# One triangular solve for both chunk pairs of an RWKV group, and the last group's solve on VectorE

## The chip, the cores and the metric

The kernel runs on one core of a Trainium2 chip. The metric is the device time of one execution in microseconds (us); lower is better. A core has a matrix engine (TensorE, PE in the profile, its weight loads PEld), three engines for elementwise work (VectorE, DVE; ScalarE, ACT; GpSimd, POOL), and an engine that issues DMAs (SyncE, SP). Each engine takes its own instructions strictly in order and waits on semaphores for the others.

## The reference

The kernel computes two layers of a backbone over 512 latent tokens and 256 context tokens, width 1024. Each layer is a half-step SwiGLU, a token mixer and another half-step SwiGLU. The mixer projects once, runs four branches (attention, bidirectional RWKV-7, pooling, a 2-D Fourier transform), and projects their concatenation. The change is in the RWKV branch, a recurrence over a 64x64 state S for each of four heads and two directions:

```
def step(S, inp):
    r_t, w_t, k_t, v_t, a_t, b_t = inp
    sa = jnp.einsum('bhvk,bhk->bhv', S, a_t)
    S = S * w_t[:, :, None, :] + sa[..., None] * b_t[:, :, None, :] + v_t[..., None] * k_t[:, :, None, :]
    y = jnp.einsum('bhvk,bhk->bhv', S, r_t) if emit else None
    return S, y
...
rw_c, finals = rwkv_mix(rwkv_prepare(zc[3], zc[4], zc[5], zc[6], p), (zero, zero), p, emit=ctx_out)
rw_l, _ = rwkv_mix(rwkv_prepare(zl[3], zl[4], zl[5], zl[6], p), finals, p, emit=True)
```

The context sequence C is run first; its final states start the latent sequence L. In the last layer the context's output isn't needed.

## The kernel before

The recurrence is computed in chunks of 64 positions. Inside a chunk the steps depend on each other through a unit triangular 64x64 matrix for each head and direction, which has to be inverted; between chunks only S is handed on. The work of a layer is cut into three groups of 256 positions: C, and L in two halves; direction 0 runs forward and direction 1 backward, so the first L group takes positions 0 to 255 forward and 256 to 511 backward (`off` is (0, 256)), the second the reverse (`off` is (256, 0)). A group has four chunks, in two pairs (`cp` 0 and 1).

Per group, `group_start` computes the decays. Per pair, `group_pair` (L907 to L985) builds the scaled vectors `AR` and `BK`, multiplies them on PE to the matrices `gram` (evicted and masked by DVE, L956), writes the negated 32x32 diagonal blocks into `NTX` (ACT, L960), and transposes keys and values into `bkT` and `uv`.

`group_solve` (L987) inverts the 32 diagonal blocks of a pair (8 head-and-chunk combinations, 2 directions, 2 blocks). `M` holds the blocks four times, on the partitions 0 to 31, 32 to 63 and so on (two DVE transposes, L998 and L1001, a copy on ACT, one on POOL). `X` in the tile `Xs` is the inverse; row t is kept by partition group t mod 4. Then 31 steps run, j from 31 down to 1, each a multiply (L1011) and an add (L1013) on the rows from j//4 on: (8 - j//4) times j elements on each partition. Each of the 62 instructions needs the one before it. They run on POOL, except in the first pair of the second L group (`late`), on DVE. Behind it, X is copied into `NTX` (L1016, ACT and POOL) and transposed (L1019, L1020, DVE), the 64x64 inverse is put together by two small products on PE (`pm1`, L1030, and `pm2`, L1047) with ACT between, and 16 small copies write it into `gram` (L1042, ACT and POOL).

`chain` (L1052) carries S through a pair's two chunks: PE computes z from S (L1068, L1071), ACT copies it to `Wz`, PE multiplies by the inverse (L1077), DVE and ACT evict `uv` (L1082, L1080), PE makes the update (L1088), DVE adds it to S and scales it (L1090, L1091), and PE, ACT and DVE make the output y (L1097 to L1105). A chain step needs the previous S and its pair's solve; 12 steps make a layer.

Attention (`attend`) is a list of pieces that `fill(n)` emits n at a time: scores psc (L1226), maxima (L1228), exponentials, transposes ppT (L1247), products po (L1253). `fill(FILL[l][nth])` takes two pieces at each of six places, `fill(100)` the rest. `rwkv_out` makes the normalised output of the branch.

The program is given to a scheduler: instructions come in program order, with a higher priority inside `with hot()`, and a timeline that the scheduler keeps for itself sets the order of each engine at build time. So where a line stands in the program decides only in part where its instruction stands in its engine's queue. In `mixer`, before: both C pairs are prepared and solved one after the other, then pooling and Fourier, then the two C chains; in the L groups, each pair is prepared, solved, and followed by two pieces of attention and the chain of the previous pair. The last pair's chain comes after the loop.

Of the kernel before, what the change touches and what calls it, by code (L numbers as in the profile page):

```python
# [13 lines left out]
ALU = mybir.AluOpType  # L14
# [35 lines left out]
FILL = ((2,) * 6, (2,) * 6)  # L50
# [3 lines left out]
class K:  # L54
# [856 lines left out]
    def group_pair(self, R, G, cp):  # L911

        nc = self.nc
        s, off, emit = G["s"], G["off"], G["emit"]
        nx = 2 if emit else 1
        AR = self.slot([128, 2, 2, 2, 2, 64], name="AR")
        BK = self.slot([128, 2, 2, 2, 2, 64], name="BK", tag="w")
        A = self.slot([128, 32, 32], name="NTX", tag="w")
        NT = A[64:96]
        ch = slice(128 * cp, 128 * cp + 128)  # L920
        cq = "p f (c q) -> p f c q"
        mul = lambda o, a, b: nc.vector.tensor_tensor(o, a, b, op=ALU.mult)
        H = {"G": G, "cp": cp, "gram": [], "A": A, "AR": AR, "late": s == "L" and off[0] and not cp}
        for d in range(2):
            D = G["D"][d]

# [13 lines left out]
            if emit:  # L940
                r = R[s, "r"]
# [5 lines left out]
            p = [self.ps([128, 2, 2, 128], "pgr", "rk") for _ in range(2)]  # L947
# [36 lines left out]
                    nc.gpsimd.tensor_tensor(D["kds"], D["kds"], D["kd"], op=ALU.add)  # L984
        return H  # L985

    def group_solve(self, H):  # L987


        nc = self.nc  # L990
        A = H["A"]
        X1T, XT, NT = A[0:32], A[32:64], A[64:96]
# [10 lines left out]
        X, tmp, Pm = XS[:, 0:256].rearrange("p (t i) -> p t i", i=32), XS[:, 256:512], XS[:, 512:768].rearrange("p (u t) -> p u t", t=32)  # L1003
        nc.gpsimd.memset(XS[:, 0:256], 0.0)
        for x in range(4):
            nc.gpsimd.memset(XS[32 * x:32 * x + 32, x:256:36], 1.0)
# [7 lines left out]
        for x in range(4):  # L1014
            eng = nc.scalar.copy if x % 2 else nc.gpsimd.tensor_copy
            eng(XT[:, :, x::4], X[32 * x:32 * x + 32].rearrange("p t i -> p i t"))  # L1016
        Xb = M[0:32].rearrange("p (x t) u -> p x t u", x=4)
        for x in range(4):
            nc.vector.transpose(Xb[:, x].rearrange(fl), X[32 * x:32 * x + 32].rearrange(fl))  # L1019
        nc.vector.transpose(X1T.rearrange(fl), XT.rearrange(fl))  # L1020

        X1T2, Xb2 = A[64:96], M[64:96].rearrange("p (x t) u -> p x t u", x=4)
        nc.scalar.copy(X1T2[:, :, 8:16], X1T[:, :, 8:16])
        nc.scalar.copy(M[64:96, :, 24:32], M[0:32, :, 24:32])
        X1, X2 = (X1T, X1T2), (Xb, Xb2)
        p = self.ps([128, 8, 32], "pm1", "sv")
        for u in range(8):
            for d in range(2):
                r = slice(64 * d, 64 * d + 32)
                nc.tensor.matmul(p[r, u], H["gram"][d][r, u, 32:64], X1[d][:, :, 8 * d + u], start=True, stop=True)  # L1030
        for d in range(2):
            r = slice(64 * d, 64 * d + 32)
            nc.scalar.mul(Pm[r], p[r], -1.0)
        for d in range(2):
            gr = H["gram"][d]
            nc.gpsimd.memset(gr[64 * d + 32:64 * d + 64, :, 0:32], 0.0)
            for b in range(2):
                us = slice(16 * b + 8 * d, 16 * b + 8 * d + 8)
                r = slice(64 * d + 32 * b, 64 * d + 32 * b + 32)
                for x in range(4):  # L1040
                    eng = nc.gpsimd.tensor_copy if x % 2 else nc.scalar.copy
                    eng(gr[r, :, 32 * b + x:32 * b + 32:4], Xb[:, x, :, us].rearrange("p t u -> p u t"))  # L1042
        p = self.ps([128, 8, 32], "pm2", "sv")
        for u in range(8):
            for d in range(2):
                r = slice(64 * d, 64 * d + 32)
                nc.tensor.matmul(p[r, u].rearrange("p (t x) -> p x t", x=4), Pm[r, u], X2[d][:, :, :, 16 + 8 * d + u], start=True, stop=True)  # L1047
        for d in range(2):
            r = slice(64 * d, 64 * d + 32)
            nc.scalar.copy(H["gram"][d][r, :, 32:64], p[r])  # L1050

    def chain(self, R, H, final):  # L1052

# [362 lines left out]
    def mixer(self, l, h, to_hC, done, last, back, nxt):  # L1416
# [41 lines left out]
        def fill(n):  # L1458
            for _ in range(n):
                next(todo, None)  # L1460
# [6 lines left out]
            att["C"] = t[:, 0]  # L1467
        todo = (x for st in emit[::-1] for x in self.attend(F, st, att))
        mixes["L", 0] = att["L"]
        prev = None  # L1470
        nth = 0
        for H in Hs:
            with hot():
                self.chain(R, H, False)
            fill(FILL[l][nth])
            nth += 1
        for s, off, em in (("L", (0, 256), True), ("L", (256, 0), True)):
            if s == "L" and off[0] == 0:
# [283 lines left out]
```

## Time and profile before

| | |
|---|---|
| three runs | 3124.56, 3129.62, 3129.33 us (median 3129.33) |
| the profiled execution, its span | 3129.89 us, 3128.1 us |
| mean granted clock of TensorE | 0.931 |
| busy share of the span: PE, DVE, ACT, POOL | 93%, 74%, 42%, 17% |
| POOL busy | 531.4 us |

The page's busy shares are averages over the whole span. Most of the span is the SwiGLU products, where POOL has little to do; POOL's work stands in two places, the mixers of the two layers. What a change in the mixers does is read from these stretches. The granted clock is 1.00 or 0.50 at any moment; a value between them is the mean over a stretch.

### The profile page before, as it was taken

Reading aid. Unit: us, or ns where it says so; the run is one execution under the profiler, and the core shown is the slowest. Engines: PE = TensorE matmul, PEld = TensorE weight load, DVE = VectorE, ACT = ScalarE, POOL = GpSimd, SP = SyncE. Lnnn points to the kernel's source line nnn. Section 1 sums busy time; section 2 is a strip of 40 time slices with the busy share of each in tenths; the row PEclk is TensorE's granted clock in tenths of the full one; section 3 lists DMA queues with packets and bytes.
Section 4 is the critical chain, followed back from the end, with each engine's and each line's share of the span. In section 5 each row is a group of like instructions: output and inputs, shape, how many; then the busy total and the mean of one; then the engine's idle time right before and its main releaser. Section 6 shows DMA issues by size and latency. Waiting matters only on the chain.

```text
span 3128.1 us, 50276 instructions
## 1 busy us (share of the span) xinstructions
PE 2910.2 (93%) x20031; PEld 2544.1 (81%) x20031; DVE 2303.3 (74%) x3989; ACT 1313.6 (42%) x2208; POOL 531.4 (17%) x1117
## 2 busy tenths in 40 slices
PE   7999999999888889999998999999999897879997
PEld 5999998787555679999987999998877565679996
DVE  7879998744666768678778889777834566797887
ACT  4433332433676354333325443332433676354443
POOL 2000002103774030000022000001112764010002
PEclk8999999999686999999999999999999677889998
DMA  6334445320001213233232344434420002033332
GB/s 237 103 116 147 135 140 167 125 66 1 30 28 36 89 60 128 95 108 102 95 122 68 103 141 142 135 122 138 146 67 1 23 29 87 34 111 101 108 109 101
DMA packets 92187, 304.60 MB, mean 97 GB/s; under 512 B 13636, under 2 KB 15920, under 8 KB 91952
## 3 DMA queue, kind: packets, MB, share of 16 engines
q1 hardware_dynamic: 91952, 301.39, 29.2%
q8 instruction: 157, 2.57, 0.3%
q14 instruction: 78, 0.64, 0.1%
HBM read 279.81 MB, written 21.54 MB: 96 GB/s over the span
## 4 chain that ended last, share of the span: by engine, by line
PE 73%; DVE 13%; ACT 7%; issue 3%; DMA 2%; POOL 2%; SPq 0%; DVEq 0%; ACTq 0%; POOLq 0%
PE pab L123 8%; PE pab L124 8%; PE pab L125 8%; PE py L123 6%; PE py L124 6%; PE py L125 6%; PE pgu L123 4%; PE pgu L124 4%; PE pgu L125 4%; PE pw L123 2%; PE pw L124 2%; PE pw L125 2%; DVE wlo L119 2%; DVE raw L420 1%; PE pwo L125 1%
## 5 line engine op out<-in xcount | busy, mean ns | idle before, releaser
L118 ACT CAST whi<-raw 128x1024 fp32r<-128x1024 f32 x488 | 507.8, 1050 | 552.5 <-PE py L125 193.1
L119 DVE TENSOR_TENSOR wlo<-raw,whi 128x1024 fp32r<-128x1024 f32 x488 | 600.6, 1239 | 125.3 <-PE py L124 25.5
L123 PE MATMUL pab<-hshi,whi 128*128 128x256 f32 x1408 | 401.3, 288 | 24.5 <-ACT hshi L118 9.7
L124 PE MATMUL pab<-hslo,whi 128*128 128x256 f32 x1408 | 404.7, 288 | 8.9 <-DVE hslo L119 8.9
L125 PE MATMUL pab<-hshi,wlo 128*128 128x256 f32 x1408 | 401.8, 287 | 1.6 <-DVE wlo L119 1.5
L524 POOL TENSOR_TENSOR acc<-acc,gate 128x512 f32<-128x512 f32 x44 | 73.6, 1695 | 1631.0 <-DMA gate<-gate 1167.1
L123 PE MATMUL pab<-h,whi 128*128 128x256 f32 x1056 | 298.7, 287 | 9.7 <-DVE eab L463 7.4
L124 PE MATMUL pab<-h,whi 128*128 128x256 f32 x1056 | 301.6, 287 | 4.6 <-POOL h L317 4.5
L123 PE MATMUL pgu<-hhiC,whi 128*128 128x256 f32 x1056 | 299.7, 284 | 2.8 <-ACT h L286 2.2
L125 PE MATMUL pab<-h,wlo 128*128 128x256 f32 x1056 | 299.9, 286 | 1.9 <-DVE wlo L119 1.9
L124 PE MATMUL pgu<-hloC,whi 128*128 128x256 f32 x1056 | 299.5, 284 | 0.0
L125 PE MATMUL pgu<-hhiC,wlo 128*128 128x256 f32 x1056 | 299.1, 283 | 0.0
L123 PEld LDWEIGHTS pab<-hshi,whi 128*128 128x128 f32 x1408 | 273.3, 196 | 29.3 <-ACT hshi L118 11.2
L123 PE MATMUL py<-whi,actL 128*128 128x512 f32 x704 | 277.2, 395 | 11.0 <-DVE acc L513 8.3
L124 PEld LDWEIGHTS pab<-hslo,whi 128*128 128x128 f32 x1408 | 275.4, 196 | 11.9 <-DVE hslo L119 11.6
L125 PEld LDWEIGHTS pab<-hshi,wlo 128*128 128x128 f32 x1408 | 274.5, 196 | 3.1 <-DVE wlo L119 2.6
L124 PE MATMUL py<-wlo,actL 128*128 128x512 f32 x704 | 276.8, 393 | 0.0
L125 PE MATMUL py<-whi,actL 128*128 128x512 f32 x704 | 274.8, 391 | 0.0
L123 PEld LDWEIGHTS pab<-h,whi 128*128 128x128 f32 x1056 | 202.8, 194 | 15.9 <-DVE eab L463 8.1
L124 PEld LDWEIGHTS pab<-h,whi 128*128 128x128 f32 x1056 | 205.3, 194 | 9.3 <-POOL h L317 6.3
L125 PEld LDWEIGHTS pab<-h,wlo 128*128 128x128 f32 x1056 | 204.8, 195 | 4.1 <-DVE wlo L119 2.5
L123 PEld LDWEIGHTS pgu<-hhiC,whi 128*128 128x128 f32 x1056 | 202.8, 192 | 6.2 <-ACT h L286 2.7
(473 smaller groups left out, 6586.8 us busy)
## 6 DMA issues: line engine op xcount, KB each, us to landing
raw<-in_w_ffn_in SPq DMA_DIRECT2D x176, 512.0 KB, 3.6
rawm<-in_w_mod SPq DMA_DIRECT2D x128, 512.0 KB, 3.7
raw<-in_w_ffn_out SPq DMA_DIRECT2D x88, 512.0 KB, 3.5
raw<-in_w_in SPq DMA_DIRECT2D x24, 512.0 KB, 4.5
back<-spill SPq DMA_DIRECT2D x44, 256.0 KB, 4.3
spill<-res SPq DMA_DIRECT2D x16, 512.0 KB, 7.3
spill<-acc SPq DMA_DIRECT2D x16, 512.0 KB, 3.3
raw<-in_w_out SPq DMA_DIRECT2D x16, 512.0 KB, 3.5
```

Source lines behind the costliest of these rows:

```text
L118: self.nc.scalar.copy(hi, src)
L119: self.nc.vector.tensor_tensor(lo, src, hi.bitcast(F32), op=ALU.subtract)
L123: nc.tensor.matmul(out, st[0], mv[0], start=start, stop=False)
L124: nc.tensor.matmul(out, st[0], mv[1], start=False, stop=False)
L125: nc.tensor.matmul(out, st[1], mv[0], start=False, stop=stop)
L420: nc.vector.tensor_tensor(o, x, y, op=ALU.subtract)
L524: nc.gpsimd.tensor_tensor(a[:, sl], a[:, sl], self.gate[s][:, sl], op=ALU.mult)
```

## The change

Both pairs of a group are solved together. `X` has 16 rows of 32 on each partition, and row t is kept by partition group t mod 2, of 64 partitions, one half of them for each pair. A step works on (16 - j//2) times j elements. `M` holds the blocks twice for each pair (one DVE transpose a pair, then ACT copies to the other 64 partitions). The small gram copies are 32x128 instead of 32x64, and half as many. The engine is an argument: POOL for C and the first L group, DVE for the second.

In the mixer the solve comes after both pairs. The C chains move into the first L group's loop, each behind a pair; each group's chains run in the next group's loop, and the last group's two chains after the loops. `fill(FILL[l][nth])` is called four times a layer.

```diff
-        M = w([128, 32, 32], "M")
-        nc.vector.transpose(M[0:32].rearrange(fl), NT.rearrange(fl))
-        nc.scalar.copy(M[32:64], M[0:32])
-        nc.gpsimd.tensor_copy(M[64:96], M[0:32])
-        nc.vector.transpose(M[96:128].rearrange(fl), NT.rearrange(fl))
+        Ms = [w([128, 32, 32], "M")]
+        M = Ms[0]
+        for cp, H in enumerate(Hs):
+            nc.vector.transpose(M[32 * cp:32 * cp + 32].rearrange(fl), H["A"][64:96].rearrange(fl))
+        nc.scalar.copy(M[64:128, 16:32], M[0:64, 16:32])
+        nc.scalar.copy(M[64:128, 0:16], M[0:64, 0:16])
...
-        eng = nc.vector if H["late"] else nc.gpsimd
         for j in range(31, 0, -1):
-            a = j // 4
-            tv = tmp[:, 0:(8 - a) * j].rearrange("p (t i) -> p t i", i=j)
-            eng.tensor_tensor(tv, M[:, j:j + 1, 0:j].to_broadcast([128, 8 - a, j]),
-                              X[:, a:8, j:j + 1].to_broadcast([128, 8 - a, j]), op=ALU.mult)
-            eng.tensor_tensor(X[:, a:8, 0:j], X[:, a:8, 0:j], tv, op=ALU.add)
-        for x in range(4):
-            eng = nc.scalar.copy if x % 2 else nc.gpsimd.tensor_copy
-            eng(XT[:, :, x::4], X[32 * x:32 * x + 32].rearrange("p t i -> p i t"))
+            a = j // 2
+            tv = tmp[:, 0:(16 - a) * j].rearrange("p (t i) -> p t i", i=j)
+            eng.tensor_tensor(tv, M[:, j:j + 1, 0:j].to_broadcast([128, 16 - a, j]),
+                              X[:, a:16, j:j + 1].to_broadcast([128, 16 - a, j]), op=ALU.mult)
+            eng.tensor_tensor(X[:, a:16, 0:j], X[:, a:16, 0:j], tv, op=ALU.add)
+        Ms.append(w([128, 32, 32], "M"))
...
+            nc.gpsimd.tensor_copy(XT[:, :, 0::2], Xc[0].rearrange("p t i -> p i t"))
+            nc.scalar.copy(XT[:, :, 1::2], Xc[1].rearrange("p t i -> p i t"))
...
             for cp in range(2):
                 Hs.append(self.group_pair(R, g, cp))
-                self.group_solve(Hs[cp])
+            self.group_solve(Hs, nc.gpsimd)
...
-        prev = None
         nth = 0
-        for H in Hs:
-            with hot():
-                self.chain(R, H, False)
-            fill(FILL[l][nth])
-            nth += 1
         for s, off, em in (("L", (0, 256), True), ("L", (256, 0), True)):
...
+            prev, Hs = Hs, []
             g = self.group_start(P, R, s, off, em, first)
             for cp in range(2):
-                H = self.group_pair(R, g, cp)
-                self.group_solve(H)
+                Hs.append(self.group_pair(R, g, cp))
                 fill(FILL[l][nth])
                 nth += 1
-                if prev:
-                    with hot():
-                        self.chain(R, prev, False)
-                prev = H
+                with hot():
+                    self.chain(R, prev[cp], False)
+            self.group_solve(Hs, nc.vector if off[0] else nc.gpsimd)
...
         with hot():
+            self.chain(R, Hs[0], False)
             rw = mixes["L", 1] = self.slot([128, 2, SEQ], name="mixL")[:]
             self.rwkv_out(P, R, "L", rw, (1, 2), "rk")
-            self.chain(R, prev, True)
+            self.chain(R, Hs[1], True)
             self.rwkv_out(P, R, "L", rw, (0, 3), "rk")
```

The instruction counts of the program fall from 1010 to 590 on POOL, from 3798 to 3783 on DVE, from 1958 to 1930 on ACT and from 17090 to 17054 on PE; SP keeps its 657.

Where the instructions stand in their engine's queue is shown at three places. A row is the instruction's number on its engine, its line, its operation and tiles (with buffer numbers), and its shape. The first is POOL in the first L group of layer 0, in the middle of the solves, before:

```order
306 L1011 TENSOR_TENSOR Xs_8292<-M_8287,Xs_8292 128x66
307 L1011 TENSOR_TENSOR Xs_8540<-M_8535,Xs_8540 128x69
308 L1013 TENSOR_TENSOR Xs_8292<-Xs_8292 128x6x11
309 L1013 TENSOR_TENSOR Xs_8540<-Xs_8540 128x3x23
310 L1011 TENSOR_TENSOR Xs_8292<-M_8287,Xs_8292 128x60
311 L1011 TENSOR_TENSOR Xs_8540<-M_8535,Xs_8540 128x66
312 L1013 TENSOR_TENSOR Xs_8292<-Xs_8292 128x6x10
```

The same place of the changed kernel, POOL in the solve of the first L group:

```order
187 L1010 TENSOR_TENSOR Xs_8260<-M_8255,Xs_8260 128x96
188 L1012 TENSOR_TENSOR Xs_8260<-Xs_8260 128x4x24
189 L1010 TENSOR_TENSOR Xs_8260<-M_8255,Xs_8260 128x115
190 L1012 TENSOR_TENSOR Xs_8260<-Xs_8260 128x5x23
191 L1010 TENSOR_TENSOR Xs_8260<-M_8255,Xs_8260 128x110
192 L1012 TENSOR_TENSOR Xs_8260<-Xs_8260 128x5x22
193 L1010 TENSOR_TENSOR Xs_8260<-M_8255,Xs_8260 128x126
```

Before, the steps of two pairs (`Xs_8292`, `Xs_8540`) alternate, so a step has another pair's step between itself and the one it needs. Now there is one solve, and each row needs the row above it.

The second place is PE in layer 0 where attention ends. Before, behind the last `po` (L1253) come the rest of the second L group's second chunk and then two chunk steps; `pch_9895` is the third chunk's z:

```order
5262 L1253 MATMUL po_10110<-pexp_10032,vqC_7588 64x128
5263 L1253 MATMUL po_10110<-pexp_10033,vqC_7588 64x128
5264 L237 MATMUL gps_10180<-ident,modC_498 8x128
5265 L1088 MATMUL pch_9820<-uv_9035,bkT_9034 64x64 x8
5266 L1097 MATMUL pch_9820<-S_859_6193,AR_8989 64x128 x2
...
5275 L1100 MATMUL pch_9820<-uv_9035,gram_9008 64x64
5276 L1068 MATMUL pch_9895<-prm_858_6192,AR_9417 64x128 x2
```

Now, behind the last `po` (L1259) come both pairs' small products of the second L group's solve (L1035, L1052) and then all four of its chunk steps; `pch_9207` is the first chunk's z:

```order
5171 L1259 MATMUL po_9804<-pexp_9726,vqC_7486 64x128
5172 L1259 MATMUL po_9804<-pexp_9727,vqC_7486 64x128
5173 L237 MATMUL gps_9874<-ident,modC_498 8x128
5174 L1035 MATMUL pm_1263_9115<-NTX_8531,gram_8548 32x32
...
5206 L1052 MATMUL pm_1264_9170<-M_9029,Xs_9034 32x2x16 x16
5207 L1052 MATMUL pm_1264_9170<-M_9100,Xs_9034 32x2x16 x16
5208 L1077 MATMUL pch_9207<-uv_8575,gram_8548 64x64
```

Four chunk steps and a solve's products stand behind attention instead of two chunk steps. In layer 1 the last `po` moves from the second L group's first chunk step into the first L group's third.

The third place is DVE in layer 0, in the solve of the second L group. Before, it is the solve of that group's first pair; in its first half it stands among the second pair's gram evictions (L956):

```order
1205 L1013 TENSOR_TENSOR Xs_9064<-Xs_9064 128x28
1206 L956 TENSOR_TENSOR gram_9436<-pgr_9426,prm_858_6192 128x512
1207 L1011 TENSOR_TENSOR Xs_9064<-M_9059,Xs_9064 128x54
1208 L956 TENSOR_TENSOR gram_9436<-pgr_9427,prm_858_6192 128x512
1209 L1013 TENSOR_TENSOR Xs_9064<-Xs_9064 128x2x27
```

Now it is the solve of both pairs; what stands between the steps is attention's maxima (L1234), the evictions of `uv` (L1088) and the updates of S (L1096, L1097) of the first L group's chain:

```order
1303 L1010 TENSOR_TENSOR Xs_9034<-M_9029,Xs_9034 128x121
1304 L1012 TENSOR_TENSOR Xs_9034<-Xs_9034 128x11x11
1305 L1010 TENSOR_TENSOR Xs_9034<-M_9029,Xs_9034 128x110
1306 L1012 TENSOR_TENSOR Xs_9034<-Xs_9034 128x11x10
1307 L1096 TENSOR_TENSOR prm_858_6192<-S_859_6193,pch_9002 64x4x64 x2
1308 L1010 TENSOR_TENSOR Xs_9034<-M_9029,Xs_9034 128x108
1309 L1097 TENSOR_TENSOR prm_858_6192<-prm_858_6192,PC_7748 64x4x64 x2
1310 L1012 TENSOR_TENSOR Xs_9034<-Xs_9034 128x12x9
```

The update with `pch_9002` is that of the first L group's fourth chunk; 18 steps of the solve stand behind it.

## Rows read from the trace of the kernel before

**Rows 1.** Busy us (count): PE, PEld, DVE, ACT, POOL, then PEclk, by stretch.
```profile
760.00:1036.00 276.00, 228.76 (x2055) 167.12 (x2056) 176.92 (x456) 179.21 (x406) 158.43 (x467) 0.74 0.08 27
2420.00:2646.00 226.00, 191.42 (x1706) 138.83 (x1705) 139.38 (x353) 155.25 (x340) 147.06 (x460) 0.71 0.08 28
```

**Rows 2.** Chain of waits, 740 to 1060 us: its shares by engine and line.
```profile
by line: PE po L1253 4.9%; PE psc L1226 4.5%; issue 3.8%; POOL Xs L1011 3.7%; POOL Xs L1013 3.6%; PE ppT L1247 3.3%; PE pw L123 2.7%; PE pw L124 2.7%; PE pw L125 2.6%; DVE gram L956 2.5%; ACT gram L1042 2.5%; ACT pexp L1232 2.4%; ACT NTX L9
```

**Rows 3.** PE's waits, 760 to 1036 us: total, times, longest us.
```profile
PE ppool L1299 <- DVE pooled L1296: 12.8, 2, 9.6
```

**Rows 4.** The tile Xs, whole span: duration ns min/median/max, first and last start.
```profile
L1011 POOL TENSOR_TENSOR Xs<-M,Xs x310: 199/293/1272, 785.4 to 2625.2; 128x60 f32<-128x60 f32 x16, 128x28 f32<-128x28 f32 x10, 128x48 f32<-128x48 f32 x10, 128x54 f32<-128x54 f32 x9
...
L1011 DVE TENSOR_TENSOR Xs<-M,Xs x62: 169/231/391, 935.9 to 2615.8; 128x60 f32<-128x60 f32 x6, 128x28 f32<-128x28 f32 x4, 128x54 f32<-128x54 f32 x4, 128x48 f32<-128x48 f32 x4
```

**Rows 5.** Timeline of POOL (start us, us, what): one solve, two solves, one solve.
```profile
798.39 0.32 POOL L1011 TENSOR_TENSOR Xs<-M,Xs 128x76 f32<-128x76 f32 x1
798.79 0.39 POOL L1013 TENSOR_TENSOR Xs<-Xs 128x76 f32<-128x76 f32 x1
...
816.78 0.51 POOL L1011 TENSOR_TENSOR Xs<-M,Xs 128x48 f32<-128x48 f32 x2
817.23 0.52 POOL L1013 TENSOR_TENSOR Xs<-Xs 128x48 f32<-128x48 f32 x2
...
874.86 0.27 POOL L1011 TENSOR_TENSOR Xs<-M,Xs 128x48 f32<-128x48 f32 x1
875.20 0.28 POOL L1013 TENSOR_TENSOR Xs<-Xs 128x48 f32<-128x48 f32 x1
```

**Rows 6.** Timeline of DVE, the solve in layer 0, first and last steps.
```profile
935.88 0.17 DVE L1011 TENSOR_TENSOR Xs<-M,Xs 128x31 f32<-128x31 f32 x1
936.09 0.19 DVE L1013 TENSOR_TENSOR Xs<-Xs 128x31 f32<-128x31 f32 x1
...
970.75 0.37 DVE L1011 TENSOR_TENSOR Xs<-M,Xs 128x28 f32<-128x28 f32 x1
...
972.65 0.17 DVE L1013 TENSOR_TENSOR Xs<-Xs 128x8 f32<-128x8 f32 x1
```

**Rows 7.** Timeline of DVE: second pairs' M transposes, C and first L group.
```profile
805.08 1.24 DVE L1001 STREAM_TRANSPOSE M<-NTX 32x1024 f32<-32x1024 f32 x1
...
886.48 1.24 DVE L1001 STREAM_TRANSPOSE M<-NTX 32x1024 f32<-32x1024 f32 x1
...
2445.00 1.24 DVE L1001 STREAM_TRANSPOSE M<-NTX 32x1024 f32<-32x1024 f32 x1
...
2524.71 1.24 DVE L1001 STREAM_TRANSPOSE M<-NTX 32x1024 f32<-32x1024 f32 x1
```

**Rows 8.** Timeline of POOL: the copy right behind a solve's last step.
```profile
845.50 1.31 POOL L1016 COPY NTX<-Xs 32x256 f32<-32x256 f32 x2
...
921.84 1.32 POOL L1016 COPY NTX<-Xs 32x256 f32<-32x256 f32 x2
...
2489.14 1.31 POOL L1016 COPY NTX<-Xs 32x256 f32<-32x256 f32 x2
```

**Rows 9.** Timeline of PE: Wz products of late chunk steps, last attention product.
```profile
946.69 0.68 PE L1077 MATMUL pch<-Wz,gram 64*64 64x64 f32 x16
...
1025.10 0.68 PE L1077 MATMUL pch<-Wz,gram 64*64 64x64 f32 x16 [2.12 <-ACT Wz L1074]
...
1034.25 0.68 PE L1077 MATMUL pch<-Wz,gram 64*64 64x64 f32 x16
1034.86 1.53 PE L1253 MATMUL po<-pexp,vqC 128*64 128x128 f32 x24
...
1048.48 0.68 PE L1077 MATMUL pch<-Wz,gram 64*64 64x64 f32 x16
...
2654.80 0.68 PE L1077 MATMUL pch<-Wz,gram 64*64 64x64 f32 x16 [0.46 <-ACT Wz L1074]
...
2669.71 0.68 PE L1077 MATMUL pch<-Wz,gram 64*64 64x64 f32 x16
```

More of the change, by code (lines that the diff above doesn't have):

```diff
@@ L922, in group_pair @@
         mul = lambda o, a, b: nc.vector.tensor_tensor(o, a, b, op=ALU.mult)
-        H = {"G": G, "cp": cp, "gram": [], "A": A, "AR": AR, "late": s == "L" and off[0] and not cp}
+        H = {"G": G, "cp": cp, "gram": [], "A": A, "AR": AR}
         for d in range(2):
@@ L985, in group_pair, with group_solve @@
         return H
-    def group_solve(self, H):
+    def group_solve(self, Hs, eng):
         nc = self.nc
-        A = H["A"]
-        X1T, XT, NT = A[0:32], A[32:64], A[64:96]
         fl = "p a b -> p (a b)"
@@ L1014, in group_solve @@
-        for x in range(4):
-            eng = nc.scalar.copy if x % 2 else nc.gpsimd.tensor_copy
-            eng(XT[:, :, x::4], X[32 * x:32 * x + 32].rearrange("p t i -> p i t"))
[L1017 to L1027, printed above, removed]
-            for d in range(2):
[L1029 to L1050, printed above, removed]
+        Ms = [w([128, 32, 32], "M")]
+        M = Ms[0]
+        for cp, H in enumerate(Hs):
+            nc.vector.transpose(M[32 * cp:32 * cp + 32].rearrange(fl), H["A"][64:96].rearrange(fl))
@@ new lines, in group_solve @@
+        nc.scalar.copy(M[64:128, 16:32], M[0:64, 16:32])
+        nc.scalar.copy(M[64:128, 0:16], M[0:64, 0:16])
+        XS = w([128, 1024], "Xs")
+        X, tmp = XS[:, 0:512].rearrange("p (t i) -> p t i", i=32), XS[:, 512:1024]
+        Pm = tmp.rearrange("p (c u t) -> p c u t", c=2, t=32)
+        nc.gpsimd.memset(XS[:, 0:512], 0.0)
+        for y in range(2):
+            nc.gpsimd.memset(XS[64 * y:64 * y + 64, y:512:34], 1.0)
+        for j in range(31, 0, -1):
+            a = j // 2
[3 more added lines that the diff above has]
+            eng.tensor_tensor(X[:, a:16, 0:j], X[:, a:16, 0:j], tv, op=ALU.add)
@@ new lines, in group_solve @@
+        Ms.append(w([128, 32, 32], "M"))
+        X1, X2, Xb = [], [], []
+        for cp, H in enumerate(Hs):
+            X1T, XT, X1T2 = [H["A"][32 * i:32 * i + 32] for i in range(3)]
+            Xc = [X[64 * y + 32 * cp:64 * y + 32 * cp + 32] for y in range(2)]
+            nc.gpsimd.tensor_copy(XT[:, :, 0::2], Xc[0].rearrange("p t i -> p i t"))
+            nc.scalar.copy(XT[:, :, 1::2], Xc[1].rearrange("p t i -> p i t"))
+            v = "p (y t) u -> p y t u"
+            Xb.append(Ms[cp][0:32].rearrange(v, y=2))
+            for y in range(2):
+                nc.vector.transpose(Xb[cp][:, y].rearrange(fl), Xc[y].rearrange(fl))
+            nc.vector.transpose(X1T.rearrange(fl), XT.rearrange(fl))
+            nc.scalar.copy(X1T2[:, :, 8:16], X1T[:, :, 8:16])
+            nc.scalar.copy(Ms[cp][64:96, :, 24:32], Ms[cp][0:32, :, 24:32])
+            X1.append((X1T, X1T2))
+            X2.append((Xb[cp], Ms[cp][64:96].rearrange(v, y=2)))
@@ new lines, in group_solve @@
+        half = [slice(64 * d, 64 * d + 32) for d in range(2)]
+        p = self.ps([128, 2, 8, 32], "pm1", "sv")
+        for cp, H in enumerate(Hs):
+            for u in range(8):
+                for d, r in enumerate(half):
+                    nc.tensor.matmul(p[r, cp, u], H["gram"][d][r, u, 32:64], X1[cp][d][:, :, 8 * d + u], start=True, stop=True)
+        for r in half:
+            nc.scalar.mul(Pm[r], p[r], -1.0)
+        for cp, H in enumerate(Hs):
+            for d in range(2):
+                gr = H["gram"][d]
+                nc.gpsimd.memset(gr[64 * d + 32:64 * d + 64, :, 0:32], 0.0)
+                for b in range(2):
+                    us = slice(16 * b + 8 * d, 16 * b + 8 * d + 8)
+                    r = slice(64 * d + 32 * b, 64 * d + 32 * b + 32)
+                    for y in range(2):
+                        cpy = nc.gpsimd.tensor_copy if y else nc.scalar.copy
+                        cpy(gr[r, :, 32 * b + y:32 * b + 32:2], Xb[cp][:, y, :, us].rearrange("p t u -> p u t"))
@@ new lines, in group_solve @@
+        p = self.ps([128, 2, 8, 32], "pm2", "sv")
+        for cp in range(2):
+            for u in range(8):
+                for d, r in enumerate(half):
+                    nc.tensor.matmul(p[r, cp, u].rearrange("p (t y) -> p y t", y=2), Pm[r, cp, u], X2[cp][d][:, :, :, 16 + 8 * d + u],
+                                     start=True, stop=True)
+        for cp, H in enumerate(Hs):
+            for d, r in enumerate(half):
+                nc.scalar.copy(H["gram"][d][r, :, 32:64], p[r, cp])
@@ L1469, in mixer @@
         mixes["L", 0] = att["L"]
-        prev = None
         nth = 0
-        for H in Hs:
-            with hot():
-                self.chain(R, H, False)
-            fill(FILL[l][nth])
-            nth += 1
         for s, off, em in (("L", (0, 256), True), ("L", (256, 0), True)):
-            if s == "L" and off[0] == 0:
+            if off[0] == 0:
                 for n in ("kds", "Y"):
```

3 lines of the change are left out of this document (removed).

## The prediction

> **What bounds the kernel now.** The page's averages mix stages with other limits, so I start from the table by stretches [rows 1]. The mixers' middle parts, where solves, chains and attention run side by side, are about 760 to 1060 us (layer 0) and 2420 to 2700 us (layer 1). Up to the last attention product TensorE (PE) is busy 228.8 of 276 us in layer 0 and 191.4 of 226 us in layer 1, at a granted clock of 0.74 and 0.71, a mix of both levels; VectorE (DVE) and ScalarE (ACT) are busy for 62 to 69%, GpSimd (POOL) for 57 to 65%. No engine is full. PE is the nearest to it, with 47 and 35 us idle. The chain of waits in layer 0 agrees [rows 2]: the solve's two lines on POOL hold 7.3% of 320 us, some 23 us; attention's products (po, psc, ppT) hold more. And 12.8 us of PE's idle time belong to a wait for the pooling branch's `pooled` [rows 3], which no edit here touches. So there are two bounds: the serial cycle "pairs, solve, chain", and PE's own work with the gaps it must have.
>
> **The solve's steps.** Before, ten solves on POOL and two on DVE make 620 and 124 step instructions, by the counts 310 and 62 for the multiply line and as many for the add [rows 4]. Afterwards four are on POOL and two on DVE, 248 and 124, each instruction longer. Row j of one kind works on (8 - j//4)·j elements before, at most 76, 1560 in a solve; on (16 - j//2)·j after, at most 136, 2856 in a solve. A step alone on POOL goes from start to start in 0.34 us at 48 elements and 0.40 at 76 [rows 5]: 0.06 us for 28 elements, about 2 ns each. With 92 elements on average (2856/31) that is 0.34 + 0.002·44 = 0.43 us a step, 27 us for 62. Inserted POOL work (copies, memsets, the `kdsL` add) adds some 4 in C and 8 in the first L group: I take 31 and 35 us. Below, a step of the 48-element length would give 62·0.34 = 21; above, if each step were lengthened by as much again as its own 0.27 (what contention did to DVE's steps, below), 62·0.70 = 43. The catch is that two solves side by side fill each other's dependency wait: two 48-element steps in 0.45 us, 0.23 each against 0.34 alone [rows 5]. The new solve is one dependent chain with nothing beside it. Two interleaved ones cost 124·0.23 to 0.28 = 29 to 35 us, one joint solve 31 to 35: on the serial path joining the two saves nothing where they overlapped. What it does save, some 60 us of POOL's busy time a layer, bounds nothing.
>
> On DVE a 31-element step took 0.17 to 0.19 us at 936 us, and a 28-element step 0.37 us at 970.75, while POOL was solving too [rows 6]. After the change no solve is left on POOL when DVE solves, so I price its steps without contention: 0.21 us at 31 elements from start to start plus about 1 ns for each of 61 more, 0.27 to 0.30, thus 18 us; the 27 other instructions that stand between the steps in layer 0's order (maxima, S updates, uv) bring it to 30. The late solve before was spread over 37 us (935.88 to 972.82) for half as much. Bounds 18 and 40.
> By the Trainium skill (SBUF — State Buffer, "Who interferes with whom"), a VectorE instruction with two SBUF inputs contends with GpSimd instructions that read SBUF. The doubled 28-element step agrees. The rule speaks for the DVE solve, and against the first two: the next pairs' two-input DVE work would run against a solve on POOL at nearly every step, and POOL's steps would be nearer 0.5 than 0.43 us, 4 us more for each of four solves; the 76-element steps, beside DVE work on two inputs, kept to 0.40, so I stay with the lower price.
>
> **The rest of a solve.** Two M transposes for a group instead of four, at 1.24 us [rows 7], save 2.5 us of DVE a group, 7.4 a layer; POOL loses its M copies, ACT and POOL have half as many small gram copies, each twice as long. These lie beside other work; I count only the DVE part, as a shorter "pairs" term.
>
> **The order.** Chain C moves into the first L group's loop, each L chain into the next group's, and the last group's both chains come after the loop. What this costs is in three places. (a) A solve starts only when both pairs are ready, and the next pairs stand behind its transposes on DVE. (b) PE's order ends attention in layer 0 before the last group's pm products; four chunk steps follow bare, where two did. In layer 1 the last attention is inside L1's last steps; one and four are bare, where three were. (c) DVE's solve is queued with the S updates of the running chain, and cannot end before that chain has.
>
> **The sum, layer 0, by the serial cycle.** C's second M transpose ends at 806.3 [rows 7]; the two new ones come in the same place, but the first pair's no longer run behind steps: 803. C solve to 834. From the end of C's last solve to L1's second M transpose before: 845.5 to 887.7 [rows 7, 8], 42 us; with both C pairs' chain steps now under `hot` in it, I take 46: 880. L1 solve 35: 915. Both L2 pairs 47: 962. DVE solve 30: 992. From solve end to the first Wz product 25 (921.8 to 946.7 [rows 8, 9]): 1017. Three more bare steps at 7 (1034.25 to 1048.48 holds two [rows 9]): 1038, where the last Wz product was at 1048.5. Gain 10.
> **By PE's work.** Up to the last attention product, PE loses two chunk steps of about 4.5 us: 228.8 - 9 = 220; with 25 to 35 of the 47 idle us kept (the pooling wait and attention's own), it ends at 1005 to 1015. Then pm1, pm2 and the first z, about 12, and 21 for the steps: 1038 to 1048. Gain 0 to 10. I take 8 between both.
> **Layer 1.** Pairs ready 2446 (its M transpose ends 2446.2), solve 31, pairs 40 (2489.1 to 2526 is 37 [rows 7, 8]), solve 35, pairs 41, solve 25, latency 25, steps 21: 2664. By PE: 182 + 22 to 32 from 2420, one bare step 4, then 33: 2661 to 2671. Before, the last Wz product ran at 2669.7, behind w_out's first products; 2654.8, the step before it, and 7 make about 2662 without them [rows 9]. Gain 1, within -9 and +8.
> Together 9 us: 3129.9 (the profiled execution; its span 3128.1 and 1.8 around it, and 0.6 above the median) - 9 = 3121.
>
> **Rivals.**
> *Slower: the tail and the serial solve decide.* For it: two POOL solves overlapped in both layers, and attention covered all but two or three steps; now DVE's solve waits for chain L1's S updates, in order. A fill of two attention steps is drawn four times, no longer six, so less of attention stands late. Priced: POOL steps 0.5 (+4 each, two a layer), the DVE solve 40 instead of 30, four steps at 9.15 instead of 7 (1025.10 to 1034.25 [rows 9]), +6: the last Wz at 1062 in layer 0 (+14), in layer 1 at 2664 + 8 + 6 = 2678 (+8). 3152; with half of that, 3141. It decides once the DVE solve ends after 1003 or 2605. Against it: before, the first Wz of L2 came 52 us after DVE's late solve had ended (1025.1 against 972.8), so that solve was not what was late.
> *Much faster: contention and gaps go.* Pairs in 37 and solves in 27 bring the cycle to 803+27+40+30+40+22+20+21 = 1003, and PE bounds: with only 15 us idle, 995 + 33 = 1028, gain 20; layer 1 gains 12. 3098. For it: DVE is relieved by 7.4 us a layer, and POOL's copies no longer wait for a solve on DVE; PE at the clock's higher level for more of the stretch would add to it. Against: PE's largest idle piece is not the solve's.
> *No change: attention's work sets the end.* PE's bound at its upper end in both layers: gain 0 and -1; 3130. For it: the po product at 1034.86 lies only 14 us before the last chain product, so before PE and the chain ended nearly together.
>
> **How the numbers follow.** What a measurement of this kernel can tell from no change is 0.2%, 6.3 us. The forecast (3115 to 3126, gain of 4 to 14) 0.40; much faster 0.15; no change 0.17; slower 0.28. Of the forecast's own 0.40 three quarters are beyond 6.3 us: faster 0.45, same 0.26, slower 0.29. The likeliest is 3121. Range: from 3095, just below the fast rival, to 3146, within the slow one.
>
> **What would show it.** DVE's solve with steps below 0.30 us and ending by 995 and 2600; POOL's joint solves 31 to 35 us from the first step to the last; last Wz product near 1040 and 2663; PE's idle time up to the last attention product below 38 and 30 us. Wrong would be: POOL steps of 0.5 and more; a DVE solve that stretches to 40 because S updates arrive late; bare chunk steps more than 8 us apart; or a granted clock in the stretch far from 0.7, which would move all PE terms at once.

## The result, and the profile after

The changed kernel takes 3110.41 us (median of four executions, 3105.82 to 3114.07) against 3129.47 us before (four, 3124.56 to 3132.51): a ratio of 0.9947, 95% interval 0.9932 to 0.9961. That is 16.6 us by the ratio, 12 to 21 by its interval. The forecast of 3121 had the direction right and half of the size. The profiled execution took 3105.82 us, span 3103.8; it is the fastest of the four, so the shifts read from it below add up to 24 us and not to 16.6.

To see in which stage the time went, I follow one event that both kernels have in the same number, the cast of a weight tile on ACT (L118, 488 times). The 121st cast stands ahead of the mixer of layer 0 and the 139th behind it, the 367th ahead of the mixer of layer 1 and the 391st behind it. Timeline of ACT in the kernel before, start and length in us:

```profile
1150.68 1.99 ACT L118 CAST whi<-raw 128x1024 fp32r<-128x1024 f32 x2 [0.16 <-DVE raw L420]
...
2771.10 2.94 ACT L118 CAST whi<-raw 128x1024 fp32r<-128x1024 f32 x3
```

The same casts in the changed kernel (the second row of each kernel begins one cast earlier, at the 390th):

```profile
1131.91 1.99 ACT L118 CAST whi<-raw 128x1024 fp32r<-128x1024 f32 x2 [0.16 <-DVE raw L420]
...
2746.69 2.94 ACT L118 CAST whi<-raw 128x1024 fp32r<-128x1024 f32 x3
```

The shift is 18.8 us behind layer 0 and 24.4 behind layer 1. At the 121st cast, ahead of the first mixer, it is 0.8, at the 367th, ahead of the second, 21.5. So layer 0's mixer gave 18.0 us, layer 1's 2.9; the other 3 are spread over the stages that the change doesn't touch.

Busy time by stretch from cast to cast (columns as in [rows 1]), layer 0 and layer 1, first of the kernel before, then of the changed one:

```profile
657.94:1150.68 492.74, 429.88 (x3188) 328.77 (x3186) 304.04 (x745) 259.12 (x534) 199.23 (x498) 0.84 0.11 38
2340.02:2772.04 432.02, 369.31 (x2757) 281.23 (x2756) 267.59 (x622) 235.24 (x468) 181.56 (x489) 0.80 0.11 37
...
657.17:1131.91 474.74, 416.27 (x3188) 320.84 (x3186) 286.90 (x727) 249.09 (x498) 140.13 (x255) 0.88 0.11 39
2318.47:2747.64 429.17, 356.44 (x2757) 275.68 (x2756) 259.84 (x604) 225.27 (x432) 123.97 (x246) 0.81 0.11 37
```

PE does the same number of products in both kernels. In layer 0 it is busy for 13.6 us less and idle for 4.4 less; in layer 1 it is busy for 12.9 less and idle for 10.0 more. So by the profile, in which the ends of products are modelled, PE's own work took 26.5 us less, more than the 21 that the two mixers gave, and PE waited 5.6 us more.

Within these stretches, the answer to [rows 1]: busy time up to the last attention product.

```profile
760.00:988.00 228.00, 198.63 (x1812) 146.69 (x1810) 142.67 (x411) 151.67 (x341) 92.25 (x214) 0.84 0.06 21
2398.50:2586.00 187.50, 158.54 (x1420) 116.09 (x1418) 110.58 (x291) 126.51 (x270) 83.48 (x207) 0.77 0.06 22
```

Attention ends at 988 where it ended at 1036. PE is busy for 198.6 us instead of 228.8 and idle for 29 instead of 47, at a granted clock of 0.84 instead of 0.74.

The solves, the answer to [rows 5, 6, 8]. POOL's timeline, C and then the first L group, first step and the copy behind the last:

```profile
799.52 0.24 POOL L1010 TENSOR_TENSOR Xs<-M,Xs 128x31 f32<-128x31 f32 x1 [7.81 <-ACT M L999]
...
831.32 2.19 POOL L1018 COPY NTX<-Xs 32x512 f32<-32x512 f32 x2
...
879.23 0.24 POOL L1010 TENSOR_TENSOR Xs<-M,Xs 128x31 f32<-128x31 f32 x1 [3.81 <-ACT M L999]
...
915.53 2.18 POOL L1018 COPY NTX<-Xs 32x512 f32<-32x512 f32 x2
```

DVE's timeline in the second L group's solve: first step, one of the longest, and the transposes behind the last.

```profile
962.59 0.19 DVE L1010 TENSOR_TENSOR Xs<-M,Xs 128x31 f32<-128x31 f32 x1 [0.66 <-ACT M L999]
...
977.91 0.30 DVE L1012 TENSOR_TENSOR Xs<-Xs 128x136 f32<-128x136 f32 x1
...
989.91 2.16 DVE L1023 STREAM_TRANSPOSE M<-Xs 32x512 f32<-32x512 f32 x3
```

They took 31.8, 36.3 and 27.3 us and began at 799.5, 879.2 and 962.6. And PE's timeline at the end of the stretch, the answer to [rows 9]: last attention product, small products, the Wz products of the last group's first three chunk steps, the first product of the output projection (`pwo`), and the Wz product of the fourth step.

```profile
986.70 0.93 PE L1259 MATMUL po<-pexp,vqC 128*64 128x128 f32 x13
994.12 0.31 PE L1035 MATMUL pm<-NTX,gram 32*32 32x32 f32 x2 [6.30 <-DVE NTX L1024]
998.65 1.10 PE L1035 MATMUL pm<-NTX,gram 32*32 32x32 f32 x32 [4.22 <-ACT NTX L1026]
...
1007.80 1.12 PE L1083 MATMUL pch<-Wz,gram 64*64 64x64 f32 x16 [0.62 <-ACT Wz L1080]
1015.76 0.68 PE L1083 MATMUL pch<-Wz,gram 64*64 64x64 f32 x16 [0.47 <-ACT Wz L1080]
1023.02 0.68 PE L1083 MATMUL pch<-Wz,gram 64*64 64x64 f32 x16 [0.53 <-ACT Wz L1080]
...
1035.64 0.65 PE L123 MATMUL pwo<-whi,mhi 128*128 128x512 f32 x1
...
1040.81 0.68 PE L1083 MATMUL pch<-Wz,gram 64*64 64x64 f32 x16
```

Behind attention PE waits for the solve: 6.3 us and 4.2 us in these rows. With attention gone early, the serial cycle is what ends last. The fourth chunk step stands among the products of the output projection. In the kernel before, the projection began behind the last Wz product (1048.48 in [rows 9]):

```profile
1053.59 0.50 PE L123 MATMUL pwo<-whi,mhi 128*128 128x512 f32 x1 [0.45 <-ACT mhi L118]
```

So layer 0's last Wz product moved by 7.7 us, and the start of the projection by 18.0, which is the gain of the layer; the projection's products then took 85 us in both kernels.

### The profile page after: what moved, and what is told of

Read it like the earlier page. It is cut to its first block, busy times and chain, and to the rows that moved or that the text cites. A ratio compares the mean times of both kernels' runs of the same rounds, so it can differ in the third digit from the quotient of the medians.

```text
span 3103.8 us, 49666 instructions
## 1 busy us (share of the span) xinstructions
PE 2882.5 (93%) x20031; PEld 2530.9 (82%) x20031; DVE 2279.7 (73%) x3953; ACT 1293.3 (42%) x2136; POOL 412.2 (13%) x631
## 5 line engine op out<-in xcount | busy, mean ns | idle before, releaser
L118 ACT CAST whi<-raw 128x1024 fp32r<-128x1024 f32 x488 | 507.9, 1050 | 560.0 <-PE py L125 194.8
L119 DVE TENSOR_TENSOR wlo<-raw,whi 128x1024 fp32r<-128x1024 f32 x488 | 601.7, 1241 | 118.0 <-PE py L124 26.9
L125 PE MATMUL pgu<-hhiC,wlo 128*128 128x256 f32 x1056 | 299.3, 284 | 0.0
L124 PEld LDWEIGHTS pab<-hslo,whi 128*128 128x128 f32 x1408 | 275.0, 195 | 12.4 <-DVE hslo L119 12.0
```

The lines of the kernel that those rows point to most:

```text
L118: self.nc.scalar.copy(hi, src)
L119: self.nc.vector.tensor_tensor(lo, src, hi.bitcast(F32), op=ALU.subtract)
L124: nc.tensor.matmul(out, st[0], mv[1], start=False, stop=False)
L125: nc.tensor.matmul(out, st[1], mv[0], start=False, stop=stop)
```

## The experiments

All ratios are to the kernel before, timed on the same chip, where it took 3126 to 3130 us; gains are read from the ratios. Where a layer is named, the time is that of the profiled execution from cast to cast, as above: before 492.7 and 432.0 us, changed 474.7 and 429.2. Theory A: the serial cycle of pairs, solves and chains sets the mixers' end, in both kernels. Theory B: attention's work on PE (with its clock) sets it. Theory C: the gain is that POOL and DVE no longer solve at once.

**All joint solves on GpSimd** (from the changed kernel).

```diff
-            self.group_solve(Hs, nc.vector if off[0] else nc.gpsimd)
+            self.group_solve(Hs, nc.gpsimd)
```

> The changed kernel with the second L group's joint solve on GpSimd too. Theory A (the serial cycle of solves and pairs sets the end): the last solve takes 31 to 33 us instead of 27, about +5 us a layer, 3120. Rival B (TensorE's attention work and its granted clock set the end, the solve is hidden): no change, 3110, or a little faster because 62 steps leave VectorE's queue.

Measured: 3113.69 us, ratio 0.9961 [0.9949, 0.9973], against 0.9947: some 4 us of the gain, with intervals that overlap. On GpSimd the last solve took 27.8 us in either layer (962.5 to 990.3 in layer 0), where 31 to 33 were expected and VectorE took 27.3 and 26.9. The edit hardly lengthened the solve, so this run doesn't decide between A and B; it shows that the choice of engine for the last solve is a small part.

**Single solves, both of the last group on VectorE** (from the kernel before).

```diff
-        H = {"G": G, "cp": cp, "gram": [], "A": A, "AR": AR, "late": s == "L" and off[0] and not cp}
+        H = {"G": G, "cp": cp, "gram": [], "A": A, "AR": AR, "late": s == "L" and off[0]}
```

> The kernel before with both pairs of the last L group solved on VectorE, each alone. Theory C (the gain is the absence of two solves on VectorE and GpSimd at once): a good part of the gain, 3115 to 3120. Theories A and B: within 4 us of before, 3126 to 3133, since 31 us of one-pair steps would stand in VectorE's queue.

Measured: 3122.73 us, ratio 0.999 [0.9982, 0.9999], 3 us. The time in which POOL and DVE solve at once falls from 25 to 10 us in layer 0, and to nothing in layer 1. Theory C falls as the main cause. This kernel is the base of the next one.

**The new order with single solves** (the row above, and the changed kernel's mixer, with a solve behind each pair).

```diff
-        for H in Hs:
-            with hot():
-                self.chain(R, H, False)
-            fill(FILL[l][nth])
-            nth += 1
...
             for cp in range(2):
-                H = self.group_pair(R, g, cp)
-                self.group_solve(H)
+                Hs.append(self.group_pair(R, g, cp))
+                self.group_solve(Hs[cp])
                 fill(FILL[l][nth])
                 nth += 1
-                if prev:
-                    with hot():
-                        self.chain(R, prev, False)
-                prev = H
+                with hot():
+                    self.chain(R, prev[cp], False)
...
```

> The changed kernel's order of chains, pairs and attention pieces with one solve for each pair as before (C and first L group on GpSimd, both pairs of the second on VectorE). If the order makes the gain: 3110 to 3115. If the joint solve makes it: 3125 to 3132.

Measured: 3118.2 us, ratio 0.9977 [0.9967, 0.9987]: 7 us in all, 4 more than the engine alone. The order is part of it, not all. By layer it took 478.8 and 432.9 us: 13.9 less than before, and 0.9 more.

**Joint solves with the C chains in their old place** (from the changed kernel).

```diff
+        for H in Hs:
+            with hot():
+                self.chain(R, H, False)
+            fill(FILL[l][nth])
+            nth += 1
...
-                with hot():
-                    self.chain(R, prev[cp], False)
+                if off[0]:
+                    with hot():
+                        self.chain(R, prev[cp], False)
```

> The joint solves, but the two C chains at their old place ahead of the L groups, with their two attention fills each: six fills a layer again. If moving the C chains makes the gain: 3122 to 3130. If the joint solve makes it: 3108 to 3114.

Measured: 3120.79 us, ratio 0.9982 [0.9974, 0.9991], 6 us. In the profiled executions layer 0 kept its gain (476.5 us), and layer 1 lost 6.7 (438.7). So joint solve and order together give more (16.6) than the sum of what each adds to the 3 us of the engine (2 and 4); by layer it is layer 1 that needs both, and in layer 0 each alone brings most of the gain. PE's busy time says what each does. With the joint solves and the C chains in their old place it is 414.6 and 353.9 us, as short as in the changed kernel, but PE is idle for 84.9 us in layer 1. With the new order and single solves it is 425.9 and 374.3, and only the idle time falls by much, to 53 and 59 (62.9 and 62.7 before). The joint solve goes with shorter busy time, the order with less waiting.

**Half of the steps left out**, in both kernels (every second step of a solve is missing, so the inverse is incomplete).

```diff
-        for j in range(31, 0, -1):
+        for j in range(31, 0, -2):
```

> The kernel before with every second step of each solve left out (16 steps of 31; the inverse is then incomplete). Theory A (the serial cycle of solves, pairs and chain sets the mixers' end): each solve is 8 to 12 us shorter, and most of it shows: 3085 to 3105. Theory B (TensorE's attention work and its clock set the end in the kernel before): less than 12 us, 3115 to 3128.

> The changed kernel with the same steps left out. Three solves a layer of 32, 32 and 27 us become about 17, 17 and 17. Theory A: 40 us a layer are taken from the cycle, at least half of it shows: 3030 to 3070. Theory B: attention ends as before and the end moves by less than 10 us a layer: 3090 to 3110.

Measured: before, 3116.51 us, ratio 0.9954 [0.9937, 0.9971], 14 us. Changed, 3084.72 us, ratio 0.9855 [0.9841, 0.987]: 29 us below the changed kernel's own 0.9947. The same cut is worth twice as much in the changed kernel. In its trace the solves are 46 us shorter in layer 0 and 43 in layer 1, and yet layer 0 gains only 1.1 us (473.6) and layer 1 19.1 (410.1). In layer 0 the scheduler has moved attention back: it ends at 1035.2, behind the last Wz product, where it ended at 988. Shorter solves alone don't shorten that layer further. In the kernel before it is the reverse: layer 0 gains 13.0, layer 1 0.4. Neither theory holds for both kernels: the one before is near B, the changed one lies between, with about a third of what its solves are shorter by.

**Without attention**, in both kernels (scores, maxima, exponentials, transposes and products are left out, and the branch's output is zeroed).

```diff
-        for u in units + [None]:
+        for u in []:
```

> The kernel before without attention's pieces (its output is zeroed; scores, maxima, exponentials, transposes and products are left out). What is left in the mixers' middle is the cycle of pairs, solves and chains. Compared with the changed kernel without them. Theory A: that one is still 12 to 20 us shorter. Theory B: 0 to 6 us.

> The changed kernel without attention's pieces. Theory A: 12 to 20 us below the kernel before without them; theory B: within 6 us of it; a third theory (without attention as cover the joint solve is a loss): 5 to 20 us above it.

Measured: before, 3054.16 us, ratio 0.9758 [0.9744, 0.9773]; changed, 3066.31 us, ratio 0.9796 [0.9782, 0.9811]. The intervals are apart: **without attention the changed kernel is the slower one, by 12 us.** The third theory holds. PE's timeline in layer 0, kernel before without attention, the first and the last Wz product of the first L group, then the first and the third of the second:

```profile
922.74 0.68 PE L1077 MATMUL pch<-Wz,gram 64*64 64x64 f32 x16 [1.06 <-ACT Wz L1074]
...
961.58 0.68 PE L1077 MATMUL pch<-Wz,gram 64*64 64x64 f32 x16
974.12 1.05 PE L1077 MATMUL pch<-Wz,gram 64*64 64x64 f32 x16
...
989.51 0.68 PE L1077 MATMUL pch<-Wz,gram 64*64 64x64 f32 x16 [0.47 <-ACT Wz L1074]
```

The changed kernel without attention:

```profile
922.99 0.68 PE L1083 MATMUL pch<-Wz,gram 64*64 64x64 f32 x16
...
948.36 1.12 PE L1083 MATMUL pch<-Wz,gram 64*64 64x64 f32 x16 [0.53 <-ACT Wz L1080]
978.11 1.12 PE L1083 MATMUL pch<-Wz,gram 64*64 64x64 f32 x16 [0.62 <-ACT Wz L1080]
...
994.09 0.83 PE L1083 MATMUL pch<-Wz,gram 64*64 64x64 f32 x16 [0.53 <-ACT Wz L1080]
```

Both begin the L groups together, at 923. The changed kernel runs its first group's four steps sooner (to 948 instead of 962) and then waits 30 us for the joint solve of the second, where the kernel before goes on after 12.5. In the bare cycle the joint solve costs time: 3.7 us in layer 0 (447.8 against 444.1) and 12.4 in layer 1 (416.8 against 404.4), less some 4 in the stages between. Attention is worth 75 us of the kernel before (3129 - 3054) and some 47 of the changed one (0.9947 - 0.9796 of 3129): the change makes the cycle longer and lets attention run beside it.

**All three joint solves on VectorE, and only the two of L** (from the changed kernel).

```diff
-            self.group_solve(Hs, nc.gpsimd)
+            self.group_solve(Hs, nc.vector)
...
-            self.group_solve(Hs, nc.vector if off[0] else nc.gpsimd)
+            self.group_solve(Hs, nc.vector)
```

(the kernel with the L groups alone has the second edit only)

> The changed kernel with all three joint solves of a layer on VectorE. If the changed kernel is bound by its serial cycle, and GpSimd's solves are slowed by and slow VectorE's work: C and L1 solves of 19 to 22 us instead of 32, some 10 us a layer: 3085 to 3100. If VectorE's queue is then the bound (18 us more of steps among the pairs' work): 3110 to 3120.

> Both L groups' joint solves on VectorE, C's on GpSimd. By the cycle: half of the gain that all three would bring, 3098 to 3106; if VectorE binds: 3108 to 3116.

Measured: all three, 3090.85 us (four executions, 3087.32 to 3100.17), ratio 0.9876 [0.9858, 0.9894], 39 us below before and 22 below the changed kernel: the best version that I ran. L alone, 3112.2 us, ratio 0.9951 [0.9937, 0.9965], nothing beside the changed kernel. The profiled execution of the kernel with all three is the slowest of its four, so the trace shows only part of the gain. DVE's timeline in it, C's solve and the first L group's, first and last step:

```profile
802.10 0.19 DVE L1010 TENSOR_TENSOR Xs<-M,Xs 128x31 f32<-128x31 f32 x1 [0.36 <-ACT M L999]
...
830.62 0.19 DVE L1012 TENSOR_TENSOR Xs<-Xs 128x16 f32<-128x16 f32 x1
...
878.21 0.19 DVE L1010 TENSOR_TENSOR Xs<-M,Xs 128x31 f32<-128x31 f32 x1 [0.60 <-ACT M L999]
...
901.81 0.19 DVE L1012 TENSOR_TENSOR Xs<-Xs 128x16 f32<-128x16 f32 x1
```

The first L group's solve takes 23.8 us instead of 36.3, C's 28.7 instead of 31.8. With the L groups alone on VectorE, the first L group's solve took 41.4 us in layer 0 (878.6 to 920.0): 86 other DVE instructions, 27.8 us by their durations, stand among its steps there, and 12, of 4.8 us, where all three are on VectorE. So that run did not get the shorter solve; why the scheduler places the work so differently is not settled by these runs.

**The last group's pairs solved one by one on VectorE**, with joint solves for the first two groups: on GpSimd, then on VectorE too (`solve_one` is `group_solve` of the kernel before, with its engine as an argument).

```diff
             for cp in range(2):
                 Hs.append(self.group_pair(R, g, cp))
+                if off[0]:
+                    self.solve_one(Hs[cp], nc.vector)
...
-            self.group_solve(Hs, nc.vector if off[0] else nc.gpsimd)
+            if not off[0]:
+                self.group_solve(Hs, nc.gpsimd)
```

> The changed kernel's order and joint solves for C and the first L group, but the second L group's pairs solved one by one on VectorE, each as soon as it is ready. If the joint solve's price is the late start of the last group (nothing covers it): the first chunk step of the last group comes some 8 us earlier a layer, 3095 to 3104. If the order of one joint chain on VectorE is as good: 3107 to 3116.

> Joint solves of C and the first L group on VectorE, the second L group's pairs solved one by one on VectorE. If the two gains (all on VectorE, ratio 0.9876; last group one by one, 0.9915 against 0.9947) are of different waits: about 0.984, 3078 to 3086. If both take away the same wait: 3088 to 3096.

Measured: with GpSimd for the first two, 3101.53 us, ratio 0.9915 [0.99, 0.9929], 10 us below the changed kernel. In layer 0 the last group's first Wz product came at 997.5 instead of 1007.8, as expected: the late start of the last group is part of the joint solve's price, as the runs without attention say. In layer 1 it did not come earlier (299.3 us behind the 367th cast, 295.3 in the changed kernel), and what gave the 2.6 us there is not shown. With VectorE for all, 3110.37 us, ratio 0.9931 [0.9918, 0.9944]: 5 us below the changed kernel. Both readings that I had named are missed; the two gains spoil each other. PE's timeline of that kernel at the end of layer 0:

```profile
1013.84 0.68 PE L1148 MATMUL pch<-Wz,gram 64*64 64x64 f32 x16
...
1033.11 0.68 PE L1148 MATMUL pch<-Wz,gram 64*64 64x64 f32 x16
1034.61 1.09 PE L1324 MATMUL po<-pexp,vqC 128*64 128x128 f32 x14
1042.54 1.82 PE L1324 MATMUL po<-pexp,vqC 128*64 128x128 f32 x24
```

Here the cycle is early, but attention (po) ends at 1044 behind the last Wz product: the other bound has come back.

## Why the prediction was right, and where its size was off

**The changed kernel's cycle: right, step by step.** The solves were to begin at 803, 880 and 962 and began at 799.5, 879.2 and 962.6; they were to take 31, 35 and 30 us and took 31.8, 36.3 and 27.3. DVE's steps were to stay below 0.30 us, and the 136-element step took 0.30. The joint solve on POOL was not slowed to 0.5 us a step by contention: with nothing between its steps it took 27.8 us (the run with all joint solves on GpSimd), where the sum of the nearest rows made 27. The contention with VectorE showed there in a few steps only (last section).

**One term of it was mis-sized, and one was missing.** From solve end to the first Wz product I took 25 us [rows 8, 9]; it is 1007.8 - 989.9 = 17.9. The 25 of the kernel before hold attention's products, which stand in PE's queue between; after attention's end nothing does. That is 7 us, but they did not reach the last chunk step. Three bare steps were to follow at 7 us; two did, 8.0 and 7.3 us apart, and the third came after 17.8, among the products of the branch's output and of the projection. So the last Wz product, which I took for the end of the layer, came at 1040.8 where 1038 was forecast, and its 7.7 us are near the 8 that I took. The layer gave 18.0, because the projection no longer stands behind that step: it began at 1035.6 instead of 1053.6. The sum had no term for the projection's start; that is the 10 us that it was short of in layer 0.

**"By PE's work" was wrong.** It had attention end at 1005 to 1015, with PE busy for 220 us and 25 to 35 us of idle time. The idle time came as said, 29; the busy time was 198.6, and attention ended at 988. Of the 30 us by which PE was busy for less than before, some 11 are products that now stand behind attention, by my estimate from the mean times of the kernel before: two chunk steps, for which I took 9, are 6 to 7 of them, and 128 small products of the last solve, for which I took nothing, the rest. The other 19 are the same products in less time: the 80 products of the scores were busy for 29.8 us instead of 38.9, at a granted clock of 0.84 instead of 0.74. A clock far from 0.7 was among the signs that the prediction would be wrong, "which would move all PE terms at once". Where the kernel before went at half clock for most of 950 to 1000 us,

```profile
950.00:1000.00 50.00, 39.07 (x365) 26.91 (x364) 34.43 (x89) 34.90 (x79) 29.38 (x90) 0.58 0.14 43
```

the changed one did a third more products in less busy time:

```profile
950.00:1000.00 50.00, 37.48 (x482) 27.94 (x479) 38.99 (x116) 35.01 (x72) 7.52 (x15) 0.88 0.04 12
```

Whether the clock is a cause here or follows from the better placed work, no run tells apart: no experiment held the order and changed the clock. It is not all of it: in layer 1's mixer PE was busy for 12.9 us less at a clock of 0.81 instead of 0.80.

That the idle time came out as said is in part luck. I had kept in it the "12.8 us" of waiting for `pooled` [rows 3], "which no edit here touches", and that wait fell to 0.5 (with 4 us of other waits of that product). Before, the M transposes of C's first pair (779.45 to 781.96) stood ahead of the first `pooled` on DVE (786.78); now the first of them comes behind it (787.53, behind 782.42), and attention's first scores start at 808.2 instead of 816.0. PE's wait in the changed kernel:

```profile
PE ppool L1305 <- DVE pooled L1302: 0.5, 1, 0.5
```

This wait is not what the layer's gain hangs on: the new order with single solves still waits 13.2 us for `pooled`, and its layer 0 is 13.9 us shorter.

**The subtraction was between two different bounds.** I took the cycle's new end from the old end, 1048.5, as if that were the cycle's too. The runs without attention and with half of the steps say that it wasn't: the old bare cycle is 12 us shorter than the new one, and halving its solves gave 14 us. What the change removes is the price of attention beside the cycle, 75 us before and some 47 after. So the direction came out right, but not for the reason given: the forecast had the serial cycle 10 us shorter, and by itself it got longer. The rival "the tail and the serial solve decide" named a real cost, and the runs without attention price it at 12 us; it didn't show as a loss because attention then ended 48 us earlier, where I had expected 21 to 31.

**Layer 1** was forecast at a gain of 1 and gave 2.9. Its last solve ended at 2595.9, which is 2617.4 with the 21.5 us that the kernel was ahead by then; 2618 was forecast. The sign that I gave beside it, "ending by 2600", didn't fit that sum, and the slower rival's threshold of 2605 lay below it too; the solve met the sign only because the kernel was ahead. (The rival "no change" adds up to 3131, not 3130; nothing hangs on it.)

## What to carry to other kernels

A serial chain and a filler on the same engine must be priced as two bounds, before and after the change, and the new end of one must not be subtracted from the old end of the other; a run without the filler shows which of them it is. The mark that stands for the end of a stage has to be one that the next stage waits for: here the last Wz product moved by 7.7 us and the next stage by 18.0. A wait in the profile that "no edit touches" can be touched when the change moves work in the queue of the engine that it waits for: here it fell from 12.8 to 0.5 us. Two gains found apart need not add up where a scheduler places the work anew: here two of 22 and 10 us came to 5.

## What the runs showed of the hardware

A VectorE instruction on two SBUF operands was held until the GpSimd instruction beside it had ended. In the kernel before, DVE's L1180 on 128x128 took 1.35 us at 784.23 and ended at 785.58; POOL's L984, 1.48 us from 783.95, ended at 785.43. Timeline of DVE:

```profile
784.23 1.35 DVE L1180 TENSOR_TENSOR zqkv<-zqkv,qkg 128x128 f32<-128x128 f32 x1
```

POOL's row beside it:

```profile
783.95 1.48 POOL L984 TENSOR_TENSOR kdsYC<-kdsYC,ga 128x512 f32<-128x512 f32 x1
```

In the changed kernel, with POOL idle (781.70 to 786.94), the same instruction took 0.28 us:

```profile
782.22 0.28 DVE L1186 TENSOR_TENSOR zqkv<-zqkv,qkg 128x128 f32<-128x128 f32 x1
```

So the contention named by the Trainium skill (SBUF — State Buffer, "Who interferes with whom") shows here on DVE's side, not only as the doubled steps of [rows 6]. I had priced it for POOL's steps, at nearly every step; it shows there too, but in 9 of the 124 steps of layer 0's two joint solves on POOL. Those took 0.57 to 0.78 us, and each of them overlapped a DVE instruction on two SBUF operands. One of 30 elements on POOL:

```profile
829.59 0.67 POOL L1010 TENSOR_TENSOR Xs<-M,Xs 128x30 f32<-128x30 f32 x1
```

and DVE beside it, which ended at 830.17, 0.09 us before the step:

```profile
829.48 0.69 DVE L895 TENSOR_TENSOR kdsL<-ga,l_k 128x512 f32<-128x512 f32 x1
```

The solve's first step, of 31 elements, took 0.24 us.
